# Conv and pooling states turned in one run of nine transposes, and last conv rows turned back by groups, in a one-core hybrid decoder step

## The chip, the core and the metric

The kernel runs on one core of a Trainium2 chip. The metric is the device time of one execution in microseconds (us). The kernel before took 1273.08 us, the median of three runs (1272.99 to 1273.53).

## What is computed

One layer of a decoder with two branches: a pooling branch, and a Mamba-2 branch with a short causal conv in front of it. There are 1024 prompt rows and 8 sequences of 8 sample rows, 1088 in all, D = 1024, everything in fp32. Each sample sequence brings the last 15 input rows of its pooling branch (`state_pool`, 8 x 15 rows of 512) and the last 3 raw rows of its conv (`state_conv`, 8 x 3 rows of 3072); the prompt brings none. Of both branches the last rows are outputs again. Cut to what matters here:

```python
def layer(x, c, pos0, pool_buf, conv_buf, ssm_state, ...):
    h = rmsnorm(x) * (1 + scale) + shift
    u_pool, z_pool, z_ssm, xbc, dt_raw, g_raw = split(h @ w_in)
    p, pool_new = pool_mix(u_pool, pool_buf, ...)   # windows 2, 4, 8, 16 over concat([pool_buf, u_pool])
    p = (p * silu(z_pool)) @ w_pool_out             # pool_new: its last 15 rows
    xbc_c, conv_new = causal_conv(xbc, conv_buf, conv_w, conv_b)   # 4 taps over concat([conv_buf, xbc])
    xs, B, C = split(silu(xbc_c))                   # conv_new: the last 3 rows of the concatenation
    y, ssm_new = ssd(xs, softplus(dt_raw + dt_bias), -exp(a_log), B, C, ssm_state)
    s = rmsnorm((y + d_skip * xs) * silu(z_ssm)) @ w_ssm_out
    x = x + gate * ((sigmoid(g0) * p + sigmoid(g1) * s) @ w_o)
```

## The kernel before

Activations stand turned: channels on the 128 partitions, rows (time) along the free axis. The product with `w_in` is made pair by pair: `pair` computes two blocks of 128 output channels for all rows by Strassen's method, seven products of two halves, each half 12 matmuls, since each fp32 operand is split into a high and a low part (L609 high times high, L610 high weight times low activation, L611 low weight times high activation). A pair is 168 matmuls of 272 columns, some 21 us of TensorE (PE). PSUM tiles come in turn from two sets, `mm` and `ps`; the `ps` set has five buffers and also takes every transpose.

The weights of a pair are loaded raw on the queue of SyncE (SP) (L541, or L544 where the two blocks don't lie side by side; tiles `rawA`, five buffers), combined on VectorE (DVE) (L555, tiles `raw`), and split by ScalarE (ACT) into the high part (`whi`, L166) and by GpSimd (POOL) into the low one (`wlo`, L169), four buffers of each.

Over a pair's matmuls lies the work of the unit that takes its results: a generator, stepped between products. The stages that matter:

- From 0 to about 95 us: `first`, in an order written by hand: modulation, norm, and the activations' halves.
- From about 95 to 545 us: the stage of the change. Its units are `to_conv` (which opens a pool of SBUF tiles, among them `GA`, seven buffers), one pair of `light` (z or gate channels), `pool_rows` (a DRAM-to-DRAM copy of old pool rows, on SP), then the pairs of `heavy` and `light` in turn: a pool pair (`upair`), then for each of four groups two x pairs, one B/C pair, and a further pool pair.
- From 545 us: dt is read back and turned (L1090 loads `s` on SP, L1109 turns it in nine transposes, one run), then the samples' recurrence beside the last `light` pairs to about 800, the chunks of the prompt to about 1160, and the tail of output products.

In the stage of the change no order is written by hand: a scheduler places instructions by its own estimate of time, engine by engine, in program order where priorities are equal. `behind(engine)` ties an instruction to a place: not ahead of the last one that the program has issued on that engine.

Beside these pairs `splits` prepares the later weights: loaded on ACT's queue (L427), scaled and copied by ACT, subtracted by POOL, the high part stored on ACT's queue, the low part on SP's (L442, `wp` and `ws`), in a place fixed by `behind(SP)`; the raw tile (`pw`) has two buffers.

`conv_unit(mc, dst)` is made for each of 24 blocks of 128 channels: 16 of x, 4 of B, 4 of C. It loads the block's 24 state rows as a 24 x 128 tile (L1033, SP, tag `stc`, four buffers), turns it on PE (L1039), and ACT copies the 24 columns (L1040) ahead of the samples' rows in a `GA` tile. When the pair's results stand there, ACT copies the last three columns of each sequence and of the prompt into `t27` (L1049 and the line behind it); ACT and DVE make the conv (L1054, L1057), ACT the Silu, and the results are stored on ACT's queue (L1064, L1065). Then PE turns the 27 columns back (L1067), ACT copies them out of PSUM (L1069), and two stores on ACT's queue (L1070, L1071) bring them to the outputs.

`u_unit(gi)` does the like for each of four pool blocks: 120 state rows loaded (L760, SP), turned (L775) and copied by DVE (L776); at the end two turns (L805 the prompt's 15 columns, L806 the samples' 64), two ACT copies and two stores on ACT's queue.

Of the kernel before, what the change touches and what calls it, by code (L numbers as in the profile page):

```python
# [20 lines left out]
P = 128  # L21
# [3 lines left out]
NB = 8  # L25
# [21 lines left out]
def tile_pool_ssd_step(  # L47
# [9 lines left out]
    def nm(s):  # L57
        uid[0] += 1
        return f"{s}_{uid[0]}"
# [36 lines left out]
    def PB():  # L96
        return psB.tile([P, 512], F32, tag="ps", name=nm("ps"))
# [38 lines left out]

    act(rc[:, 0:1], eps, AF.Silu)
    nc.gpsimd.memset(rc[:, 0:1], 1.0)
    vb = sm.tile([44, P], F32, tag="stc", name="vb", bufs=4)
    store_(vb[0:16, :], b_ada[0, 0:2048].rearrange("(m p) -> m p", p=P))  # L140
    store_(vb[16:24, :], norm_g[0].rearrange("(m p) -> m p", p=P))
    store_(vb[24:40, :], ssm_norm_g[0].rearrange("(m p) -> m p", p=P))
# [227 lines left out]
    cvT = pa.tile([P, 120], F32, tag="cvT", name="cvT")  # L370

    def late_loads():
        va = sm.tile([120, P], F32, tag="stc", name="va", bufs=4)
        load(va[0:96, :], conv_w[0].rearrange("k (m p) -> (k m) p", p=P))
        load(va[96:120, :], conv_b[0].rearrange("(m p) -> m p", p=P))
        V.memset(dtb, 0.0)
        load(dtb[0:NH, 0:1], dt_bias[0].rearrange("(h o) -> h o", o=1))
        dk = sm.tile([16, 2], F32, tag="rsm", name="dk")
        load(dk, d_skip[0].rearrange("(m h) -> m h", h=2))
        yield  # L380
        dx = sm.tile([16, 2, 64], F32, tag="stc", name="dx", bufs=4)
# [374 lines left out]

    def u_unit(gi):
        L = gi + 1
        stp = sm.tile([120, P], F32, tag="stc", name=nm("stp"), bufs=4)
        load(stp, state_pool[0, :, :, gi * P:(gi + 1) * P].rearrange("b t c -> (b t) c"))  # L760
        pwt = sm.tile([P, P], F32, tag="stc", name=nm("pwt"), bufs=4)
        load(pwt, pool_w[0, gi])
        yield
        up = GA([P, CW_])
        us = small([P, NB, 23], "us", 1)

        def done(o, n, comb, buf):
            e = min(o + n, SEQ) - o
            comb(up[:, 15 + o:15 + o + e], 0, e)
            if e < n:  # L770
                comb(us[:, :, 15:23], e, n, lambda t: t.rearrange("p (b t) -> p b t", t=8))
        yield done
        V.memset(up[:, 0:15], 0.0)
        ps = PB()
        nc.tensor.transpose(ps[:, :120], stp, ident[:120, :120])  # L775
        V.tensor_copy(us[:, :, 0:15], ps[:, :120].rearrange("p (b t) -> p b t", t=15))  # L776
        u64 = sm.tile([P, NB, 8], F32, tag="rsm", name=nm("u64"))
        act(u64, us[:, :, 15:23], AF.Copy)
        u15 = sm.tile([P, 27], F32, tag="t27", name=nm("u15"))
        act(u15[:, 0:15], up[:, SEQ:SEQ + 15], AF.Copy)  # L780
        yield
        a, av = up, us
        ab = [GA([P, T]) for _ in range(2)]
        for l in range(L):
            st = 1 << l
            o0 = 2 * st - 1
            b = ab[l % 2]
# [17 lines left out]
        nc.tensor.transpose(ps[:15, :P], u15[:, 0:15], ident)  # L805
        nc.tensor.transpose(ps[:NS, P:2 * P], u64.rearrange("p b t -> p (b t)"), ident)  # L806
        o15, o64 = [sm.tile([n, P], F32, tag="o27", name=nm("o15")) for n in (15, NS)]
        act(o15, ps[:15, :P], AF.Copy)
        act(o64, ps[:NS, P:2 * P], AF.Copy)
        store_(new_pool_p[0, 0, :, gi * P:(gi + 1) * P], o15)  # L810
        store_(new_pool_s[0, :, 7:15, gi * P:(gi + 1) * P], o64)
        y = up[:, :T]
        for o, n in BLK:
            ps = PB()
            mm(ps[:, :n], pwt, d[:, o:o + n], start=True, stop=True)
            act(y[:, o:o + n], ps[:, :n], AF.Copy, scale=pscl[:, gi:gi + 1])
        yp_[gi] = y
        yield 1
# [209 lines left out]

    def conv_unit(mc, dst):
        stc = sm.tile([24, P], F32, tag="stc", name=nm("stc"), bufs=4)
        load(stc, state_conv[0, :, :, mc * P:(mc + 1) * P].rearrange("b t c -> (b t) c"))  # L1033
        yield
        rp = GA([P, CW_])
        seg = rp[:, SEQ + 3:CW_].rearrange("p (b t) -> p b t", t=11)
        V.memset(rp[:, 0:3], 0.0)
        ps = PB()
        nc.tensor.transpose(ps[:, :24], stc, ident[:24, :24])  # L1039
        act(seg[:, :, 0:3], ps[:, :24].rearrange("p (b t) -> p b t", t=3), AF.Copy)  # L1040

        def done(o, n, comb, buf):
            e = min(o + n, SEQ) - o
# [1 line left out]
            if e < n:  # L1045
                comb(seg[:, :, 3:11], e, n, lambda t: t.rearrange("p (b t) -> p b t", t=8))
        yield done
        t27 = sm.tile([P, 27], F32, tag="t27", name=nm("t27"))
        act(t27[:, 0:24].rearrange("p (s t) -> p s t", t=3),  # L1049
            rp[:, SEQ:SEQ + 88].rearrange("p (s t) -> p s t", t=11)[:, :, 0:3], AF.Copy)  # L1050
        act(t27[:, 24:27], rp[:, SEQ + 88:SEQ + 91], AF.Copy)
# [11 lines left out]
        act(s64, d[:, SEQ + 3:CW_].rearrange("p (b t) -> p b t", t=11)[:, :, 0:8], AF.Silu)  # L1063
        store_(dst[:, :SEQ], d[:, :SEQ])  # L1064
        store_(dst[:, SEQ:], s64.rearrange("p b t -> p (b t)"))  # L1065
        ps = PB()
        nc.tensor.transpose(ps[:27, :P], t27, ident)  # L1067
        o27 = sm.tile([27, P], F32, tag="o27", name=nm("o27"))
        act(o27, ps[:27, :P], AF.Copy)  # L1069
        store_(new_conv_p[0, 0, :, mc * P:(mc + 1) * P], o27[0:3])  # L1070
        store_(new_conv_s[0, :, :, mc * P:(mc + 1) * P], o27[3:27])  # L1071
        yield 1

    H0B = 4
# [478 lines left out]
    def to_conv():  # L1553
        nonlocal right
        right.__exit__(None, None, None)
        right = tc.tile_pool(name="ga", bufs=1, side="right", reuse_waits="tile")
        gas.append(right.__enter__())

    def to_ssd():
        nonlocal right, sd, sp, mask, maskS, blkS, dtT, acT, wdT, wd3, blk3, Elb  # L1560
# [20 lines left out]
            load(new_pool_s[0, :, 0:7, :], state_pool[0, :, 8:15, :])  # L1581

    first()
    units = [plain(to_conv), light[1], plain(pool_rows)]
    units += weave(heavy, light[2:-LAST])
    pre = splits()
    units.append(plain(lambda: [None for _ in pre]))
# [262 lines left out]

    def m_split(k, mem):

        sh = sm.tile([P, P], F32R, tag="stc", name=nm("sh"), bufs=4)
# [201 lines left out]
```

## Time and profile before

| what | before |
|---|---|
| median of three runs | 1273.08 us |
| profiled execution | 1271.29 us |
| its span in the trace | 1269.5 us |
| PE busy | 1242.3 us, 98% |
| DVE, ACT, POOL busy | 900.9, 718.0, 683.1 us |
| DMA | 234.90 MB, mean 185 GB/s |
| granted clock, mean | 0.997 |
| PE rows that turn states or last rows | 24 + 24 + 4 + 8 = 60 |

The span is what the trace covers; the execution's own time is 1.8 us more, and the median of the unprofiled runs another 1.8. Busy times are sums of durations without overlaps, so an engine at 98% has hardly a gap; the table by stretches says where its gaps lie. Rows of matmuls give start, duration, engine, line and shape; matmuls overlap, so a duration is more than what one instruction takes from the engine. The profile counts some matmul rows less than the program has (9771 of them are in the trace).

### The profile page before, as it was taken

How to read it: one execution, taken by the hardware profiler on the slowest of the kernel's cores; microseconds unless marked ns; L12 is line 12 of the kernel's file. 1: busy time of each engine (PE TensorE's matmuls, PEld its weight loads, DVE VectorE, ACT ScalarE, POOL GpSimd, SP SyncE). 2: the span in 40 equal slices, each digit the busy share in tenths (PEclk: the TensorE clock that was granted, in tenths of full speed). 3: DMA queues.
4: the chain of work that ended last, by engine and by line, in shares of the span. 5: the costliest groups of instructions: out<-in, count | busy, mean ns of one | idle time of the engine just before them, and what ended most of it. 6: DMA issues, size and time to landing. Idle time of an engine off the chain costs nothing. (4 is left out here: it accounts for less than half of the span.)

```text
span 1269.5 us, 26341 instructions
## 1 busy us (share of the span) xinstructions
PE 1242.3 (98%) x9771; PEld 1173.9 (92%) x9771; DVE 900.9 (71%) x1584; ACT 718.0 (57%) x1683; POOL 683.1 (54%) x555
## 2 busy tenths in 40 slices
PE   7999999999999999999999999999999999999997
PEld 6779999999999999998989999999999999999786
DVE  4695678966979588975756665598677879766543
ACT  4665356474666656554554554687887768522211
POOL 1007669886878777764344454365565646545000
PEclk9999999999999999999999999999999999999999
DMA  9937354565456454443557445899766567485431
GB/s 332 298 104 226 116 167 161 181 204 160 138 182 201 146 182 164 149 138 116 157 142 226 151 147 167 283 300 319 217 200 201 181 212 206 152 291 179 149 108 50
DMA packets 225729, 234.90 MB, mean 185 GB/s; under 512 B 30369, under 2 KB 177009, under 8 KB 225594
## 3 DMA queue, kind: packets, MB, share of 16 engines
q1 hardware_dynamic: 155808, 159.01, 40.3%
q10 hardware_dynamic: 69794, 74.22, 17.4%
q8 instruction: 77, 1.26, 0.4%
q14 instruction: 50, 0.41, 0.1%
HBM read 158.67 MB, written 74.62 MB: 184 GB/s over the span
## 5 line engine op out<-in xcount | busy, mean ns | idle before, releaser
L169 POOL TENSOR_TENSOR wlo<-rawA,whi 128x512 fp32r<-128x512 f32 x120 | 189.0, 1580 | 170.5 <-ACT whi L166 95.8
L169 POOL TENSOR_TENSOR wlo<-raw,whi 128x512 fp32r<-128x512 f32 x92 | 155.1, 1693 | 122.2 <-ACT whi L166 119.3
L360 PE MATMUL mm<-Y,whi 128*128 128x352 f32 (+1 forms) x480 | 159.8, 333 | 0.7
L361 PE MATMUL mm<-Y,whi 128*128 128x352 f32 (+1 forms) x480 | 157.3, 328 | 0.4 <-DVE Y L1516 0.4
L362 PE MATMUL mm<-Y,wlo 128*128 128x352 f32 (+1 forms) x480 | 156.8, 327 | 0.0
L609 PE MATMUL mm<-Y,whi 128*128 128x272 f32 x496 | 146.3, 295 | 2.2 <-ACT whi L166 2.2
L611 PE MATMUL mm<-Y,wlo 128*128 128x272 f32 x496 | 143.5, 290 | 2.5 <-POOL wlo L169 2.0
L609 PE MATMUL ps<-Y,whi 128*128 128x272 f32 x496 | 143.8, 290 | 0.0
L610 PE MATMUL ps<-Y,whi 128*128 128x272 f32 x496 | 143.0, 288 | 0.0
L610 PE MATMUL mm<-Y,whi 128*128 128x272 f32 x496 | 142.9, 288 | 0.0
L611 PE MATMUL ps<-Y,wlo 128*128 128x272 f32 x496 | 142.5, 287 | 0.0
L1057 DVE SCALAR_TENSOR_TENSOR GA<-GA,cvT,GA 128x1112 f32<-128x1112 f32 x72 | 126.6, 1763 | 0.1
L166 ACT ACTIVATE whi<-rawA 128x512 fp32r<-128x512 f32 x125 | 78.1, 627 | 81.1 <-PE ps L610 44.0
L166 ACT ACTIVATE whi<-raw 128x512 fp32r<-128x512 f32 x96 | 58.9, 627 | 97.6 <-DVE raw L555 51.7
L609 PEld LDWEIGHTS mm<-Y,whi 128*128 128x128 f32 x496 | 93.5, 189 | 4.2 <-ACT whi L166 2.8
L611 PEld LDWEIGHTS mm<-Y,wlo 128*128 128x128 f32 x496 | 93.5, 189 | 2.9 <-POOL wlo L169 2.2
L360 PEld LDWEIGHTS mm<-Y,whi 128*128 128x128 f32 x480 | 90.3, 188 | 4.2 <-DVE G L1890 2.4
L610 PEld LDWEIGHTS mm<-Y,whi 128*128 128x128 f32 x496 | 93.5, 189 | 0.7 <-issue 0.6
L610 PEld LDWEIGHTS ps<-Y,whi 128*128 128x128 f32 x496 | 93.3, 188 | 0.4
L609 PEld LDWEIGHTS ps<-Y,whi 128*128 128x128 f32 x496 | 93.3, 188 | 0.2
L611 PEld LDWEIGHTS ps<-Y,wlo 128*128 128x128 f32 x496 | 93.4, 188 | 0.0
L361 PEld LDWEIGHTS mm<-Y,whi 128*128 128x128 f32 x480 | 90.3, 188 | 2.6 <-DVE Y L1516 0.9
(464 smaller groups left out, 3821.9 us busy)
## 6 DMA issues: line engine op xcount, KB each, us to landing
rawA<-in_w_in SPq DMA_DIRECT2D x46, 512.0 KB
dec<-acs_d SPq DMA_DIRECT2D x32, 512.0 KB
xbc<-GA ACTq DMA_DIRECT2D x24, 512.0 KB
xb<-xbc SPq DMA_DIRECT2D x32, 384.0 KB
rawA<-in_w_in SPq DMA_DIRECT2D x32, 256.0 KB
pw<-in_w_ssm_out ACTq DMA_DIRECT2D x32, 256.0 KB
ws<-ph ACTq DMA_DIRECT2D x32, 256.0 KB
ws<-pw SPq DMA_DIRECT2D x32, 256.0 KB
```

What stands on the lines that cost most here:

```text
L166: ins = act(hi[:, :, :ncols], raw[:, :, :ncols], AF.Copy)
L169: (eng or nc.gpsimd).tensor_tensor(lo[:, :, :ncols], raw[:, :, :ncols], hi[:, :, :ncols].bitcast(F32), ALU.subtract)
L360: mm(ps[:, :n], a, rh[k][:, o:o + n], start=(k == 0), stop=False)
L361: mm(ps[:, :n], a, rl[k][:, o:o + n], start=False, stop=False)
L362: mm(ps[:, :n], b, rh[k][:, o:o + n], start=False, stop=(k == nk - 1))
L609: mm(p, hi, ah, start=(k == 0), stop=False)
L610: mm(p, hi, al, start=False, stop=False)
L611: mm(p, lo, ah, start=False, stop=(k == 3))
L1057: V.scalar_tensor_tensor(d[:, :n], rp[:, k:k + n], cvT[:, 24 * k + mc:24 * k + mc + 1], d[:, :n], ALU.mult, ALU.add)
```

## The change

The states are no longer loaded by blocks of channels. In `to_conv` each state is loaded whole, into a `GA` tile: seen as rows of 128 channels, `state_conv` has 8 x 3 x 24 = 576 rows and `state_pool` 8 x 15 x 4 = 480, and 128 rows at a time stand on the partitions (four DMAs on SP, behind what SP has by then). A new unit `turn_states` behind the first `light` pair turns them in nine transposes (four of 128 rows and one of 64; three of 128 and one of 96) into three PSUM tiles, and ACT copies these into `st576` and `st480`, which stay. A `conv_unit` takes its 24 columns from `st576` by one strided ACT copy, a `u_unit` its 120 from `st480` by one strided DVE copy. The tag `stc` has three buffers instead of four.

The last rows: in `u_unit` the 15 and the 64 columns stand in one tile, `u79`, turned at once, copied at once, and stored by two stores on ACT's queue as before. In `conv_unit` the 27 columns of a group's six blocks stand side by side in one tile; the last of the six turns them in two transposes (108 and 54 columns), with an ACT copy each, and the twelve stores go to SP's queue, each pair of them behind what SP has been given by then, one pair per step.

The diff, without four further lines that only set `bufs=3` for `stc`:

```diff
@@ u_unit
-        stp = sm.tile([120, P], F32, tag="stc", name=nm("stp"), bufs=4)
-        load(stp, state_pool[0, :, :, gi * P:(gi + 1) * P].rearrange("b t c -> (b t) c"))
-        pwt = sm.tile([P, P], F32, tag="stc", name=nm("pwt"), bufs=4)
+        pwt = sm.tile([P, P], F32, tag="stc", name=nm("pwt"), bufs=3)
...
-        ps = PB()
-        nc.tensor.transpose(ps[:, :120], stp, ident[:120, :120])
-        V.tensor_copy(us[:, :, 0:15], ps[:, :120].rearrange("p (b t) -> p b t", t=15))
-        u64 = sm.tile([P, NB, 8], F32, tag="rsm", name=nm("u64"))
-        act(u64, us[:, :, 15:23], AF.Copy)
-        u15 = sm.tile([P, 27], F32, tag="t27", name=nm("u15"))
-        act(u15[:, 0:15], up[:, SEQ:SEQ + 15], AF.Copy)
-        yield
+        V.tensor_copy(us[:, :, 0:15], pool_t[0].rearrange("p (b t m) -> p b t m", t=15, m=4)[:, :, :, gi])
+        yield
+        u79 = sm.tile([P, 79], F32, tag="u79", name=nm("u79"), bufs=1)
+        act(u79[:, 15:].rearrange("p (b t) -> p b t", t=8), us[:, :, 15:23], AF.Copy)
+        act(u79[:, 0:15], up[:, SEQ:SEQ + 15], AF.Copy)
...
-        nc.tensor.transpose(ps[:15, :P], u15[:, 0:15], ident)
-        nc.tensor.transpose(ps[:NS, P:2 * P], u64.rearrange("p b t -> p (b t)"), ident)
-        o15, o64 = [sm.tile([n, P], F32, tag="o27", name=nm("o15")) for n in (15, NS)]
-        act(o15, ps[:15, :P], AF.Copy)
-        act(o64, ps[:NS, P:2 * P], AF.Copy)
-        store_(new_pool_p[0, 0, :, gi * P:(gi + 1) * P], o15)
-        store_(new_pool_s[0, :, 7:15, gi * P:(gi + 1) * P], o64)
+        nc.tensor.transpose(ps[:79, :P], u79, ident)
+        o79 = sm.tile([79, P], F32, tag="o79", name=nm("o79"), bufs=1)
+        act(o79, ps[:79, :P], AF.Copy)
+        store_(new_pool_p[0, 0, :, gi * P:(gi + 1) * P], o79[0:15])
+        store_(new_pool_s[0, :, 7:15, gi * P:(gi + 1) * P], o79[15:79])
@@ conv_unit
+    t27s = {}
...
-        stc = sm.tile([24, P], F32, tag="stc", name=nm("stc"), bufs=4)
-        load(stc, state_conv[0, :, :, mc * P:(mc + 1) * P].rearrange("b t c -> (b t) c"))
...
-        ps = PB()
-        nc.tensor.transpose(ps[:, :24], stc, ident[:24, :24])
-        act(seg[:, :, 0:3], ps[:, :24].rearrange("p (b t) -> p b t", t=3), AF.Copy)
+        act(seg[:, :, 0:3], conv_t[0].rearrange("p (b t m) -> p b t m", t=3, m=24)[:, :, :, mc], AF.Copy)
...
-        t27 = sm.tile([P, 27], F32, tag="t27", name=nm("t27"))
+        g, i = (mc // 4, mc % 4) if mc < 16 else (mc % 4, mc // 4)
+        if not i:
+            t27s[g] = sm.tile([P, 6 * 27], F32, tag="t27", name=nm("t27"))
+        t27 = t27s[g][:, 27 * i:27 * i + 27]
...
-        ps = PB()
-        nc.tensor.transpose(ps[:27, :P], t27, ident)
-        o27 = sm.tile([27, P], F32, tag="o27", name=nm("o27"))
-        act(o27, ps[:27, :P], AF.Copy)
-        store_(new_conv_p[0, 0, :, mc * P:(mc + 1) * P], o27[0:3])
-        store_(new_conv_s[0, :, :, mc * P:(mc + 1) * P], o27[3:27])
+        if i == 5:
+            ps = PB()
+            o27 = sm.tile([108, 2 * P], F32, tag="o27", name=nm("o27"))
+            for c, n in ((0, 108), (1, 54)):
+                nc.tensor.transpose(ps[:n, c * P:c * P + P], t27s[g][:, 108 * c:108 * c + n], ident)
+                act(o27[:n, c * P:c * P + P], ps[:n, c * P:c * P + P], AF.Copy)
+            for j, m in enumerate((4 * g, 4 * g + 1, 4 * g + 2, 4 * g + 3, 16 + g, 20 + g)):
+                r, c = j % 4 * 27, j // 4 * P
+                with behind(mybir.EngineType.SP):
+                    load(new_conv_p[0, 0, :, m * P:(m + 1) * P], o27[r:r + 3, c:c + P])
+                    load(new_conv_s[0].rearrange("b t c -> (b t) c")[:, m * P:(m + 1) * P], o27[r + 3:r + 27, c:c + P])
+                yield
@@ to_conv
+        for src, rows in ((state_conv, 576), (state_pool, 480)):
+            flat = src[0].rearrange("b t (m p) -> (b t m) p", p=P)
+            st, full = GA([P, 5, P]), rows // P
+            with behind(mybir.EngineType.SP):
+                load(st[:, :full], flat[:full * P].rearrange("(a r) p -> r a p", r=P))
+            with behind(mybir.EngineType.SP):
+                load(st[:rows - full * P, full], flat[full * P:])
+            states.append((st, rows))
+
+    def turn_states():
+        for (st, rows), kept_in in zip(states, (conv_t, pool_t)):
+            out = small([P, rows], "st%d" % rows, 1)
+            for a in range(0, rows, 512):
+                ps = PB()
+                e = min(rows, a + 512)
+                for r in range(a, e, P):
+                    n = min(P, e - r)
+                    nc.tensor.transpose(ps[:, r - a:r - a + n], st[:n, r // P], ident[:n, :n])
+                act(out[:, a:e], ps[:, :e - a], AF.Copy)
+            kept_in.append(out)
+    states, conv_t, pool_t = [], [], []
...
-    units = [plain(to_conv), light[1], plain(pool_rows)]
+    units = [plain(to_conv), light[1], plain(turn_states), plain(pool_rows)]
```

How this moves instructions is shown at three places. The first is PE between the first `light` pair and the pool pair behind it: `ps` and `mm` are PSUM tiles, `Y` the activations' halves, `whi` and `wlo` the split weights. Before:

```order
L609 MATMUL ps_1590<-Y_484,whi_1349 128x272
L610 MATMUL ps_1590<-Y_485,whi_1349 128x272
L611 MATMUL ps_1590<-Y_484,wlo_1350 128x272
L609 MATMUL mm_1632<-Y_484,whi_1315 128x272
L610 MATMUL mm_1632<-Y_485,whi_1315 128x272
L611 MATMUL mm_1632<-Y_484,wlo_1316 128x272
```

The same place of the changed kernel, where `GA_1301` holds the conv state and `GA_1304` the pool state:

```order
L610 MATMUL ps_1594<-Y_485,whi_1353 128x272
L611 MATMUL ps_1594<-Y_484,wlo_1354 128x272
L1575 MATMUL ps_1617<-ident,GA_1301 128x128 x4
L1575 MATMUL ps_1623<-ident,GA_1301 128x64
L1575 MATMUL ps_1627<-ident,GA_1304 128x128 x3
L1575 MATMUL ps_1627<-ident,GA_1304 128x96
L609 MATMUL mm_1649<-Y_484,whi_1321 128x272
L610 MATMUL mm_1649<-Y_485,whi_1321 128x272
```

The nine turns stand in one run between two pairs; the turns inside the units (L1039 and L775 of before) are gone, and the rest of the order here is that of before.

The second place is SP's queue in about the first 100 us, where the states are loaded in the changed kernel; `gate_d` is a store of the modulation, `rawA` are raw weights of `w_in`, and the last row is the copy of `pool_rows`:

```order
L760 DMA pwt_3996<-in_pool_w 128x128
L850 DMA gate_d<-bg 9x256 x4
L544 DMA rawA_1318<-in_w_in 128x4x128 x2
L541 DMA rawA_1634<-in_w_in 128x4x256
L1562 DMA GA_1301<-in_state_conv 128x4x128
L1564 DMA GA_1301<-in_state_conv 64x128
L1562 DMA GA_1304<-in_state_pool 128x3x128
L1564 DMA GA_1304<-in_state_pool 96x128
L442 DMA wp_177<-pw_1389 128x512
L1602 DMA out<-in_state_pool 8x3584
```

The four loads stand behind the two `rawA` loads; before, the first small state loads stood ahead of `gate_d`, and nothing stood between `rawA` and L442.

The third place is SP's queue at the end of the stage, where the last group's rows go out. Before (`s` is dt, `hst` the first chunk's input):

```order
L442 DMA ws_216<-pw_7176 128x512
L541 DMA rawA_7481<-in_w_in 128x4x256
L541 DMA rawA_7798<-in_w_in 128x4x256
L541 DMA rawA_7800<-in_w_in 128x4x256
L1090 DMA s_7465<-dts_d 128x1024
L1091 DMA s_7466<-dts_d 128x64
L1094 DMA A<-in_a_log 128x32
L1226 DMA hst_8140<-xbc_169 128x6x64
```

In the changed kernel, from the last of the six pairs of stores on (the other five stand right ahead of it):

```order
L1069 DMA out<-o_1114_7226 3x128
L1070 DMA out<-o_1114_7226 24x128
L1090 DMA s_7268<-dts_d 128x1024
L1091 DMA s_7269<-dts_d 128x64
L1094 DMA A<-in_a_log 128x32
L541 DMA rawA_7603<-in_w_in 128x4x256
L1226 DMA hst_7943<-xbc_169 128x6x64
L541 DMA rawA_7903<-in_w_in 128x4x256
```

The twelve stores stand ahead of the dt loads, and one of the weight loads that stood ahead of these now stands behind them.

More of the change, by code (lines that the diff above doesn't have):

```diff
@@ L138, in tile_pool_ssd_step @@
     nc.gpsimd.memset(rc[:, 0:1], 1.0)
-    vb = sm.tile([44, P], F32, tag="stc", name="vb", bufs=4)
+    vb = sm.tile([44, P], F32, tag="stc", name="vb", bufs=3)
     store_(vb[0:16, :], b_ada[0, 0:2048].rearrange("(m p) -> m p", p=P))
@@ L372, in late_loads @@
     def late_loads():
-        va = sm.tile([120, P], F32, tag="stc", name="va", bufs=4)
+        va = sm.tile([120, P], F32, tag="stc", name="va", bufs=3)
         load(va[0:96, :], conv_w[0].rearrange("k (m p) -> (k m) p", p=P))
@@ L380, in late_loads @@
         yield
-        dx = sm.tile([16, 2, 64], F32, tag="stc", name="dx", bufs=4)
+        dx = sm.tile([16, 2, 64], F32, tag="stc", name="dx", bufs=3)
         V.tensor_copy(dx, dk.unsqueeze(2).to_broadcast([16, 2, 64]))
@@ L1851, in m_split @@
     def m_split(k, mem):
-        sh = sm.tile([P, P], F32R, tag="stc", name=nm("sh"), bufs=4)
+        sh = sm.tile([P, P], F32R, tag="stc", name=nm("sh"), bufs=3)
         act(sh[:, 0:NS], acc[k][:, SEQ:], AF.Copy)
```

## The prediction

> **What bounds the kernel now.** I read the page's busy table first, then the table by stretches, then the waits of SP. The busy table has TensorE (PE) at 98% of the span; that is an average, so the stretches decide.
>
> ```profile
> PE 1242.3 (98%) x9771; PEld 1173.9 (92%) x9771; DVE 900.9 (71%) x1584; ACT 718.0 (57%) x1683; POOL 683.1 (54%) x555
> ```
> ```profile
> 95.00:145.00 50.00, 50.00 (x401) 49.83 (x400) 28.15 (x53) 24.34 (x51) 34.18 (x25) 1.00 0.55 174
> 145.00:540.00 395.00, 395.00 (x3111) 389.34 (x3111) 319.78 (x476) 231.29 (x554) 308.14 (x180) 1.00 0.52 169
> 540.00:800.00 260.00, 254.13 (x2204) 244.60 (x2203) 164.32 (x394) 135.24 (x288) 123.44 (x105) 0.99 0.53 158
> ```
>
> All edits lie between 95 and about 545 us. There PE is busy for 50.00 of 50.00 and 395.00 of 395.00 us, at a granted clock of 1.00, while ACT works 231.29 us, DVE 319.78 and POOL 308.14. So an instruction taken from PE there is taken from the time, whole, as long as nothing new makes PE wait; time taken from ACT, DVE or SP is worth nothing by itself. After that PE idles 5.9 us up to 800.
>
> A busy share does not price an instruction, because matmuls overlap. The price is the distance from start to start. In an undisturbed run of the main products:
>
> ```profile
> 181.04 0.29 PE L611 MATMUL mm<-G,wlo 128*128 128x272 f32 x1
> ...
> 189.05 0.29 PE L609 MATMUL ps<-Y,whi 128*128 128x272 f32 x1
> ```
>
> These two rows are 64 matmuls apart: 8.01 / 64 = 0.125 us each, though each "lasts" 0.29.
>
> **What leaves PE.** The counts of each kind (L806 runs as often as L805, right behind it):
>
> ```profile
> L1039 PE MATMUL ps<-ident,stc x24: 213/226/238, 144.8 to 496.8; 24*128 24x24 f32 x24
> L1067 PE MATMUL ps<-ident,t x24: 271/271/272, 177.7 to 539.4; 128*27 128x128 f32 x24
> L775 PE MATMUL ps<-ident,stp x4: 266/267/268, 144.6 to 451.3; 120*128 120x120 f32 x4
> L805 PE MATMUL ps<-ident,u x4: 271/272/272, 166.2 to 466.9; 128*15 128x128 f32 x4
> ```
> ```profile
> 169.99 0.29 PE L611 MATMUL mm<-Y,wlo 128*128 128x272 f32 x1
> 170.21 0.30 PE L1039 MATMUL ps<-ident,stc 24*128 24x24 f32 x2
> ...
> 170.79 0.29 PE L611 MATMUL mm<-Y,wlo 128*128 128x272 f32 x1
> ```
>
> Left out here are one L609 and one L610, so from L611 to L611 it would be 3 x 0.125 = 0.375 us without the pair of conv state turns (L1039); it is 0.80, so a pair costs 0.425. In the same way around one turn of the last conv rows (L1067), and between two turns of the pool rows:
>
> ```profile
> 177.55 0.29 PE L611 MATMUL ps<-Y,wlo 128*128 128x272 f32 x1
> 177.67 0.27 PE L1067 MATMUL ps<-ident,t 128*27 128x128 f32 x1
> ...
> 178.03 0.29 PE L611 MATMUL mm<-R,wlo 128*128 128x272 f32 x1
> ```
> ```profile
> 166.17 0.27 PE L805 MATMUL ps<-ident,u 128*15 128x128 f32 x1
> 166.28 0.27 PE L806 MATMUL ps<-ident,u 128*64 128x128 f32 x1
> ```
>
> 0.48 - 0.375 = 0.105 for the conv rows, 0.11 for a pool turn; L775, a pool state turn of 120 rows, I price like these. The narrow 24-row turns are thus the dear ones, 0.21 each. Sum removed: 12 x 0.425 = 5.10, 24 x 0.105 = 2.52, 4 x 0.11 = 0.44, 8 x 0.11 = 0.88; together **8.9 us**.
>
> **What comes to PE**: nine state turns (L1575 of the changed kernel), eight turns of the last conv rows (L1064) and four of the pool rows, 21 in all. The nearest existing row is nine turns in one run, eight of them 128 wide:
>
> ```profile
> 551.67 0.29 PE L610 MATMUL mm<-G,whi 128*128 128x272 f32 x1
> 551.80 1.14 PE L1109 MATMUL ps<-ident,s 128*128 128x128 f32 x9
> ...
> 553.03 0.29 PE L611 MATMUL ps<-R,wlo 128*128 128x272 f32 x1
> ```
>
> 1.36 - 0.375 = 0.985 us, 0.11 each. Two of the nine state turns have short blocks (64 and 96 rows). Their form is not in the trace; the nearest is the 24-row pair, which costs 0.425 - 2 x 0.11 = 0.2 us over its two turns' plain price. Bounds: 0 (short rows cost nothing) to 0.4 (both pay it); I take 0.2, as only the 64-row block is half empty. So 9 x 0.11 + 0.2 = 1.2; 8 x 0.11 = 0.9; 4 x 0.11 = 0.4; together **2.5 us**, bounds 2.3 to 2.7. Net: 8.9 - 2.5 = **6.4 us off PE**.
>
> [...]
>
> ```profile
> L1067 PEld LDWEIGHTS ps<-ident,t x24: 103/103/103, 177.6 to 539.3; 128*27 128x27 f32 x24
> L1109 PEld LDWEIGHTS ps<-ident,s x9: 111/141/142, 551.7 to 552.6; 128*128 128x128 f32 x8, 128*64 128x64 f32 x1
> ```
>
> The load does grow, 103 to 141 ns, but the starts stay 0.11 us apart in both, so it hides; I charge nothing and keep 21 x 0.038 = 0.8 us as a rival.
>
> **Off the path.** ACT copies: 24 of 27 rows become 8, eight pool copies out of PSUM become four, three state copies are new, and the 24 small conv copies stay with another source; DVE keeps its four pool copies. ACT and DVE have over 160 and 70 us free in 145 to 540, which covers them; without it, by the copies' own kind (L652 below, 0.39 us for 272 columns), the three state copies of 512, 64 and 480 columns would be under 2 us. They hold three of the five PSUM buffers of their kind until ACT has them out, and the two blocks hold two of the seven GA buffers until PE has turned them; both are free again long before the units that follow need them, since the first pair of conv units stands a whole unit (21 us) later.
>
> The state loads stand on SP behind a weight load that is issued here, and PE reaches their turns where the first row of the next unit stands:
>
> ```profile
> 98.94 0.37 SPq L541 DMA_DIRECT2D rawA<-in_w_in  x1
> ```
> ```profile
> 123.60 0.29 PE L609 MATMUL mm<-Y,whi 128*128 128x272 f32 x1
> ```
>
> 24 us for half a MB, so PE should not wait. ACT loses 48 store issues and SP gains them, losing 28 small loads and getting four large: 24 more issues net. One costs about this much, on either queue:
>
> ```profile
> 225.30 0.34 ACTq L1071 DMA_DIRECT2D out<-o  x1
> ```
>
> Twelve stores are 4.1 us of SP, with a wait for ACT's copy ahead; behind them stand weight loads. Their cover:
>
> ```profile
> 241.23 0.40 SPq L541 DMA_DIRECT2D rawA<-in_w_in  x1
> ```
> ```profile
> 270.75 0.68 DVE L555 TENSOR_TENSOR raw<-rawA,rawA 128x512 f32<-128x512 f32 x1
> ```
>
> The load at 241.23 is the one ahead of which the first group's stores come; by the order of before, the DVE row at 270.75 is the first to read what it brings, 29.5 us later. A burst of 4.1 us, or twice that, is hidden. If that cover were gone, a burst would cost up to its 4.1 us.
>
> The tight place is the last group, whose stores now come ahead of the loads for dt:
>
> ```profile
> 523.50 22.34 SPq L541 DMA_DIRECT2D rawA<-in_w_in  x3
> 545.94 0.45 SPq L1090 DMA_DIRECT2D s<-dts_d  x1
> ```
> ```profile
> 543.98 0.39 ACT L652 ACTIVATE s<-ps 128x272 f32<-128x272 f32 x1
> ```
> ```profile
> 548.00:550.00 2.00, 2.00 (x18) 2.00 (x17) 0.60 (x2) 0.63 (x1) 1.70 (x5) 1.00 1.05 392
> ```
>
> In the clock of before: the last group is turned where the last L1067 stands, at 539.4, and copied by ACT within a us; eight stores follow to about 543.5; the second copy stands on ACT behind L652 (ends 544.4) and two store issues (0.7), so it ends at 545.4; four stores, 1.4; then the dt load at 546.8 instead of 545.9. But the 512 KB weight load that went just ahead of it now goes behind, which at 392 GB/s is 1.3 us. It lands no later, and L1109 at 551.80 does not wait. What is late next, if so, is that weight load, by some 3 us, with the cover above.
>
> **The sum.** The profiled execution took 1271.29 us for a span of 1269.5; 1271.29 - 6.4 = 1264.9. The median of the runs shown, 1273.08, is 1.8 above it, and 1273.08 - 6.4 = **1266.7 us**, 0.5% less. 0.2% is 2.5 us, about what a measurement of this kernel can tell from no change; the bound lies at 1270.5.
>
> **Rivals.** That the change doesn't do what it says is none here: the order has the 60 turns gone and the 21 in place.
> - The last group's chain is late. For: the second copy waits on ACT behind Silu work that itself waits for DVE. Against: the order of loads. If dt comes 3 us late PE stands 3 us at L1109: 1269.7, at the edge of the bound. Chance 0.10.
> - The wide loads show: 6.4 - 0.8 = 5.6, so 1267.5. Chance 0.06.
> - More: one PE wait of 2.0 us sits at 600.9, where POOL is behind.
>
> ```profile
> PE mm L611 <- POOL wlo L169: 2.0, 1, 2.0
> ```
>
>   If the shifted stage meets it better: 1264.7. Chance 0.07.
> - The gain is swallowed behind 545, where PE already has 5.9 us of waits: the samples' chain is started by loads on SP, which do not move up with PE if SP is later. The waits then grow by what PE gained, less some: 1272, no change. Against: PE is full until 600. Chance 0.10.
> - Slower: ACT is held, not SP. A later load of raw weights on ACT's queue needs a buffer that an SP store frees; in the second group that SP store now stands behind the twelve. ACT stands in order, and what it stands before are the weight splits.
>
> ```profile
> L169 POOL TENSOR_TENSOR wlo<-rawA,whi 128x512 fp32r<-128x512 f32 x120 | 189.0, 1580 | 170.5 <-ACT whi L166 95.8
> ```
> ```profile
> ACT whi L166 <- PE ps L610: 68.0, 55, 4.8
> ```
>
>   ACT's splits wait for PE to free one of four buffers, 55 times, and run then; so three products of 24 matmuls (9 us) are the cover, less 1.6 for POOL's subtraction and about 1 for the split: it decides from a stop of 6.4 us. If all four groups stopped ACT so that PE lost the 4.1 us of a burst each: 16.4 - 6.4 = 10 us more, 1283. Chance 0.09.
>
> **How the numbers follow.** Forecast 0.58. Faster by over 0.2%: 0.58 + 0.06 + 0.07 + half of 0.10 = 0.76; within 0.2%: 0.05 + 0.10 = 0.15; slower 0.09. Range: below it reaches the extra gain and a us of scatter, 1263.5; above it takes in the late chain and the swallowed gain, 1273.5; it leaves out the slow case and scraps.
>
> **What would show it.** PE still full in 95 to 545, with 21 turns in that stretch; the nine L1575 in one run at 0.11 with no idle before them; L1109 about 6 us earlier without a wait; L1109's dt load issued some 1 us nearer to it. Wrong would be: a wait of PE for L1575's loads or dt, a DVE wait for a weight load, or the steps after 600 at their old times.

## The result, and the profile after

The changed kernel takes 0.9966 of the time of the kernel before, with a 95% interval of 0.9954 to 0.9978: medians of twelve runs each, 1270.00 us against 1274.25, so 4.3 us less (2.8 to 5.9). Two later measurements of both kernels gave 0.9951 (0.9934 to 0.9968) and 0.9965 (0.9949 to 0.9980). Forecast were 6.4 us less; the time lies in the range, and faster was forecast with 0.76.

The busy row of the page after, and the table by stretches (columns: the stretch, its length, then busy time and instructions of PE, PEld, DVE, ACT and POOL, the granted clock, DMA share and GB/s):

```profile
PE 1238.8 (98%) x9732; PEld 1173.2 (93%) x9732; DVE 907.8 (72%) x1584; ACT 715.8 (56%) x1666; POOL 683.7 (54%) x555
```
```profile
145.00:540.00 395.00, 395.00 (x3122) 392.21 (x3121) 329.69 (x477) 231.42 (x539) 315.95 (x183) 1.00 0.51 167
540.00:800.00 260.00, 253.22 (x2194) 243.47 (x2193) 165.31 (x396) 134.34 (x285) 120.86 (x104) 0.99 0.53 161
```

PE is still busy for all of 145 to 540, so the new turns and stores brought it no wait of note there. To read the stage itself, take its two ends in each trace: the row at which the states are turned, or would be, and the first turn of dt. Between them every variant but `rows_act` has the same 3290 main products. After:

```profile
124.49 0.29 PE L611 MATMUL ps<-Y,wlo 128*128 128x272 f32 x1
124.62 1.36 PE L1575 MATMUL ps<-ident,GA 128*128 128x128 f32 x9
125.76 0.37 PE L609 MATMUL mm<-Y,whi 128*128 128x272 f32 x1
125.97 0.29 PE L610 MATMUL mm<-Y,whi 128*128 128x272 f32 x1
...
546.65 1.03 PE L1109 MATMUL ps<-ident,s 128*128 128x128 f32 x8
```

546.65 - 124.62 = 422.03 us; before it was 551.80 - 123.60 = 428.20 (rows of the prediction). The stage is 6.2 us shorter. The nine state turns cost 125.97 - 124.49 = 1.48, less two plain starts of 0.125: 1.23. Three of the nine rows by themselves:

```profile
125.14 0.27 PE L1575 MATMUL ps<-ident,GA 64*128 64x64 f32 x1
```
```profile
125.35 0.33 PE L1575 MATMUL ps<-ident,GA 128*128 128x128 f32 x1
```
```profile
125.73 0.25 PE L1575 MATMUL ps<-ident,GA 96*128 96x96 f32 x1
```

From the first turn at 124.62 to the one behind the 64-row block (125.35) five starts take 0.73 us instead of 5 x 0.108 = 0.54; the three from there to the 96-row block take 0.38 instead of 0.33. The 96-row block stands 0.24 us ahead of the L610 behind it (125.97), as the plain turn at 177.67 of the prediction does (178.03 - 0.125 = 177.91). So the 64-row block costs some 0.25 us more than a plain turn and the 96-row block nothing more. One turn of a group's last rows, in the same way:

```profile
232.89 0.29 PE L611 MATMUL ps<-Y,wlo 128*128 128x272 f32 x1
233.02 0.27 PE L1064 MATMUL ps<-ident,t 128*108 128x128 f32 x1
...
233.25 0.29 PE L610 MATMUL mm<-Y,whi 128*128 128x272 f32 x1
```

0.36 - 0.25 = 0.11 us for 108 columns. The one turn that is left of each pool block stands 0.11 us ahead of the next matmul too. SP's end of the stage, on its own queue:

```profile
541.26 0.30 SPq L1070 DMA_DIRECT2D out<-o  x1
541.67 0.35 SPq L1090 DMA_DIRECT2D s<-dts_d  x1
...
543.07 0.38 SPq L541 DMA_DIRECT2D rawA<-in_w_in  x1
```

The dt load goes out 546.65 - 541.67 = 4.98 us ahead of its turn, before 551.80 - 545.94 = 5.86; PE does not wait for it.

But the span shrank by only 1.6 us in this pair of profiles. The head is part of that: the stage begins at 124.62 instead of 123.60, and ahead of that PE's order is that of before. Behind the stage more is lost. The first turn of the chunks, before and after:

```profile
810.01 0.29 PE L118 MATMUL ps<-identR,xb 128*128 128x128 f32 x2
```
```profile
806.26 0.22 PE L118 MATMUL ps<-identR,xb 128*128 128x128 f32 x1
```

It comes 810.01 - 806.26 = 3.75 us earlier, 4.77 with the head's 1.02 taken out; so 1.4 of the 6.2 went in the samples' stage. About as much again went near 1110, where eleven products in a row take (1113.56 - 1110.03) / 11 = 0.32 us each; in before products of this width start 0.17 us apart (1121.44 to 1121.61, for one).

```profile
1110.03 0.53 PE L360 MATMUL mm<-Y,whi 128*128 128x384 f32 x1
...
1113.56 0.39 PE L362 MATMUL mm<-Y,wlo 128*128 128x384 f32 x1
```

In the samples' stage one wait stands out, for the product `dec` (L1275, a subtraction on DVE), before and after:

```profile
629.53 0.50 PE L1291 MATMUL ps<-dec,dec 96*128 96x512 f32 x1 [0.64 <-DVE dec L1275]
```
```profile
621.84 0.28 PE L610 MATMUL mm<-G,whi 128*128 128x272 f32 x1
624.77 0.50 PE L1291 MATMUL ps<-dec,dec 96*128 96x512 f32 x1 [2.65 <-DVE dec L1275]
...
626.18 0.43 PE L609 MATMUL mm<-G,whi 128*128 128x272 f32 x1
...
628.68 0.43 PE L611 MATMUL ps<-Y,wlo 128*128 128x272 f32 x1
629.07 0.29 PE L610 MATMUL ps<-Y,whi 128*128 128x272 f32 x1
```

PE waits 2.65 us, and the starts behind the wait stand (628.68 - 626.18) / 11 = 0.227 us apart instead of 0.125: thirteen products at about half speed, 1.3 us more. The granted clock (third number from the end) reads 0.50 there and 1.00 ahead of the wait:

```profile
615.00:622.00 7.00, 6.86 (x56) 6.52 (x54) 3.23 (x7) 2.34 (x7) 0.65 (x2) 1.00 0.67 204
626.00:628.00 2.00, 2.00 (x11) 2.00 (x10) 1.46 (x6) 0.37 (x1) 0.00 (x0) 0.50 0.27 86
```

I took this for the place where the gain goes (theory A below). The head and the stretch near 1110 I took for chance.

### The profile page after: what moved, and what is told of

Read it like the earlier page. It is cut to its first block, busy times and chain, and to the rows that moved or that the text cites. A ratio compares the mean times of both kernels' runs of the same rounds, so it can differ in the third digit from the quotient of the medians.

```text
span 1267.9 us, 26167 instructions
## 1 busy us (share of the span) xinstructions
PE 1238.8 (98%) x9732; PEld 1173.2 (93%) x9732; DVE 907.8 (72%) x1584; ACT 715.8 (56%) x1666; POOL 683.7 (54%) x555
## 3 DMA queue, kind: packets, MB, share of 16 engines
q8 instruction: 77, 1.26, 0.4%
## 5 line engine op out<-in xcount | busy, mean ns | idle before, releaser
L169 POOL TENSOR_TENSOR wlo<-rawA,whi 128x512 fp32r<-128x512 f32 x120 | 193.6, 1619 | 159.9 <-ACT whi L166 80.4
L169 POOL TENSOR_TENSOR wlo<-raw,whi 128x512 fp32r<-128x512 f32 x92 | 149.4, 1630 | 125.4 <-ACT whi L166 83.7
L611 PE MATMUL mm<-Y,wlo 128*128 128x272 f32 x496 | 143.9, 291 | 1.8 <-POOL wlo L169 1.3
L610 PE MATMUL ps<-Y,whi 128*128 128x272 f32 x496 | 143.3, 289 | 0.0
L611 PE MATMUL ps<-Y,wlo 128*128 128x272 f32 x496 | 143.1, 288 | 0.0
L610 PE MATMUL mm<-Y,whi 128*128 128x272 f32 x496 | 142.5, 288 | 0.0
L166 ACT ACTIVATE whi<-rawA 128x512 fp32r<-128x512 f32 x125 | 78.0, 626 | 84.4 <-PE ps L610 46.6
L166 ACT ACTIVATE whi<-raw 128x512 fp32r<-128x512 f32 x96 | 58.8, 627 | 81.3 <-DVE raw L555 51.5
L611 PEld LDWEIGHTS mm<-Y,wlo 128*128 128x128 f32 x496 | 93.2, 188 | 2.4 <-POOL wlo L169 1.5
L610 PEld LDWEIGHTS mm<-Y,whi 128*128 128x128 f32 x496 | 93.5, 188 | 0.7 <-issue 0.6
L610 PEld LDWEIGHTS ps<-Y,whi 128*128 128x128 f32 x496 | 93.6, 189 | 0.4
L611 PEld LDWEIGHTS ps<-Y,wlo 128*128 128x128 f32 x496 | 93.4, 188 | 0.0
```

The source lines that it names most:

```text
L166: ins = act(hi[:, :, :ncols], raw[:, :, :ncols], AF.Copy)
L169: (eng or nc.gpsimd).tensor_tensor(lo[:, :, :ncols], raw[:, :, :ncols], hi[:, :, :ncols].bitcast(F32), ALU.subtract)
L610: mm(p, hi, al, start=False, stop=False)
L611: mm(p, lo, ah, start=False, stop=(k == 3))
```

## Experiments

**The two kernels once more, unchanged** (`again_before`, `again_after`), to know what one program's profiles differ by.

> The kernel before, unchanged, once more: what two executions of one program differ by. Theory A (the change takes about 6.2 us out of the stretch up to the turns of dt, 2 us of that go to a longer PE wait for the samples' DVE product near 622 us, and the rest of the small profiled difference of 1.65 us is chance: a head that was 1.0 us slower and a stretch of matmuls at half speed near 1110 us that cost 1.6): ratio 1.000 within 0.002; from the row of PE where the states would be turned to the first turn of dt 428.2 us within 0.3; the head up to there differs from the first profile by up to 1 us. Rival B (the profiled difference is what the change is worth, all of it structural): the head and the places of half speed are those of the first profile of before within 0.2 us.

> The changed kernel, unchanged, once more. Theory A: 422.0 us within 0.3 from the first turn of the states to the first turn of dt, 6.2 less than before; the PE wait for the samples' DVE product near 622 us is there again at some 2.6 us (before 0.6), since nothing in it is chance; the half-speed stretch near 1110 us is gone or elsewhere; ratio 0.9966 again, 0.9955 to 0.998. Rival B: the same 1.6 us are lost near 1110 us, and the ratio lies at 0.9987.

Before: ratio 0.9999 (0.9979 to 1.0020); the stage is 554.15 - 125.78 = 428.37, so the head ended 2.2 us later than in the first profile and the stage agrees to 0.2. After: 0.9951 (0.9934 to 0.9968); 545.25 - 123.22 = 422.03 again, and 2.65 us of wait near 622 again, while before has 0.40. There is no half-speed stretch near 1110 this time. Rival B falls: the 1.65 us of the first pair was a poor measure. Theory A stood, for now.

**Each part alone.** `states_only` keeps the last rows' code of before, `rows_only` the states' code of before:

```diff
 states_only, conv_unit against the changed kernel:
-        if not i:
-            t27s[g] = sm.tile([P, 6 * 27], F32, tag="t27", name=nm("t27"))
-        t27 = t27s[g][:, 27 * i:27 * i + 27]
+        t27 = sm.tile([P, 27], F32, tag="t27", name=nm("t27"))
...
+        nc.tensor.transpose(ps[:27, :P], t27, ident)
 rows_only, conv_unit against the changed kernel:
+        load(stc, state_conv[0, :, :, mc * P:(mc + 1) * P].rearrange("b t c -> (b t) c"))
...
+        nc.tensor.transpose(ps[:, :24], stc, ident[:24, :24])
```

> The states loaded whole and turned in one run, the last rows turned back block by block as before. Theory A, by the terms of the prediction (12 pairs of narrow turns at 0.425 and 4 pool state turns at 0.11 go, nine at 1.2 in all come): 5.10 + 0.44 - 1.2 = 4.3 us off the stretch up to the turns of dt, 423.9 instead of 428.2; ratio 0.9965 to 0.998. Rival C (the wide turns or the wait for the large loads cost what the narrow ones did): 427 to 428, ratio 0.9995.

> The last rows turned back by groups and stored from SP, the states loaded and turned as before. Theory A: 2.52 + 0.88 - 0.88 - 0.44 = 2.1 us off the stretch up to the turns of dt, 426.1 instead of 428.2; ratio 0.998 to 0.9995. Rival D (the twelve stores on SP delay the dt load or ACT's weights): less than 1 us off, or a wait of PE at the turns of dt.

Their stages, from the turns of the states (or the product that stands there) to the turns of dt:

```profile
124.71 0.27 PE L1569 MATMUL ps<-ident,GA 128*128 128x128 f32 x1
...
549.37 0.27 PE L1103 MATMUL ps<-ident,s 128*128 128x128 f32 x1
```
```profile
125.43 0.28 PE L609 MATMUL mm<-Y,whi 128*128 128x272 f32 x1
...
552.17 0.27 PE L1117 MATMUL ps<-ident,s 128*128 128x128 f32 x1
```

`states_only`: 424.66, 3.5 us off where 4.3 was expected; `rows_only`: 426.74, 1.5 off where 2.1 was. In the first, the one PE wait of the stage takes 0.4 us of the difference (PE for POOL's L169). Ratios: 0.9965 (0.9948 to 0.9982) and 0.9998 (0.9981 to 1.0014). The states are the larger part, as the terms had it; C and D fall for the stage. What `rows_only` gained there did not show in its time, for which 0.998 to 0.9995 was expected, though its interval reaches there: it too waited 2.44 us for `dec`.

**Why PE waits for `dec`.** The trace of after shows a chain. On DVE, L1275 stands behind a copy (L1284) for the next group, which waits for that group's load; POOL runs two weight splits (L169) at that moment:

```profile
622.29 0.65 DVE L1284 COPY cz<-hst 128x32 f32<-128x32 f32 x1 [0.88 <-DMA hst<-xbc]
622.97 1.75 DVE L1275 TENSOR_TENSOR dec<-xw,dec 32x512 fp32r<-32x512 f32 x1
```
```profile
621.63 1.27 POOL L169 TENSOR_TENSOR wlo<-rawA,whi 128x512 fp32r<-128x512 f32 x1 [6.35 <-ACT whi L166]
622.91 1.26 POOL L169 TENSOR_TENSOR wlo<-raw,whi 128x512 fp32r<-128x512 f32 x1
```

And in before:

```profile
628.42 0.34 DVE L1284 COPY cz<-hst 128x32 f32<-128x32 f32 x1 [1.22 <-DMA hst<-xbc]
628.79 0.68 DVE L1275 TENSOR_TENSOR dec<-xw,dec 32x512 fp32r<-32x512 f32 x1
```
```profile
627.44 1.28 POOL L169 TENSOR_TENSOR wlo<-rawA,whi 128x512 fp32r<-128x512 f32 x1 [4.90 <-ACT whi L166]
628.88 1.73 POOL L169 TENSOR_TENSOR wlo<-raw,whi 128x512 fp32r<-128x512 f32 x1 [0.16 <-ACT whi L166]
```

The same subtraction takes 0.68 us where it starts ahead of POOL's second split (which then takes 1.73) and 1.75 where it starts 0.06 us behind it, ending 0.55 us after POOL does. Who comes first hangs on ACT: in before POOL's second split waited 0.16 us for its high part (L166), in `again_before` 0.40 us, and DVE started in that gap; in all eight profiles with the long wait POOL's second split follows its first within 0.02 us. The longer subtraction is only part of the wait, 1.75 - 0.68 = 1.07 us of the 2.65. The rest is that DVE comes to the subtraction late: in after 0.85 us behind the time at which PE is ready for it (622.97 against 621.84 + 0.28 = 622.12), in before 0.10 us ahead (628.79 against 629.53 - 0.64 = 628.89). So two edits, each in the place of the wait. `cz_behind` keeps that copy behind its own group (and `cz_behind_before` does so in the kernel before); `sub_pool` gives the subtraction to POOL, in whose order it stands ahead of the two splits:

```diff
 cz_behind, cz_behind_before:
+            with behind(mybir.EngineType.DVE, 1):
                 V.tensor_copy(cz[:, :, 0:8], ...)
 sub_pool:
-            V.tensor_tensor(xh[64:96], xsf[64:96], xh[64:96].bitcast(F32), ALU.subtract)
+            nc.gpsimd.tensor_tensor(xh[64:96], xsf[64:96], xh[64:96].bitcast(F32), ALU.subtract)
```

> The changed kernel, with the copy of C's columns kept behind the DVE instruction that its own group issued ahead of it, so that the DVE product that PE waits for near 622 us no longer stands behind a copy of the next group, which waits for its load. Theory A (part of the gain is swallowed there: PE arrives earlier, DVE is held by that copy and then by POOL's split, PE waits 2.65 us instead of 0.4 to 0.64 and after it runs its matmuls at half speed for another 1.5 to 4 us): the wait falls to under 1.6 us, no half-speed stretch follows, and the kernel takes 2 to 4 us less than the changed one, some 1266; ratio to the kernel before 0.9915 to 0.994. Rival E (the wait is set elsewhere, by the chain of products ahead of it or by POOL alone): the wait stays within 0.4 of 2.65 and the time within 1 us of the changed kernel's.

> The same edit in the kernel before. Theory A: PE waits only 0.4 to 0.64 us there, so the edit is worth at most that: ratio 0.999 to 1.0005. If it is worth as much here as in the changed kernel (0.997 or less), the copy is a loss of both kernels and no part of why the change gained less than its turns.

> The changed kernel, with the subtraction that PE waits for near 622 us made by POOL instead of DVE, in POOL's order ahead of the two weight splits between which it was caught. Theory A: POOL is idle for 6 us ahead of them, so the product is ready about 622 us, PE waits less than 1 us there and does not slow down: 2 to 4 us less than the changed kernel, unless POOL's splits, some 1 us later each of eight times, hold PE elsewhere. Rival E: no change of that wait.

In `cz_behind` the wait is gone (0.9 us at the longest), so what Rival E says of it falls. But the time is 0.9948 (0.9931 to 0.9964), against the changed kernel's 0.9951 in the measurement before, so the 2 to 4 us of theory A did not come either. The waits of PE in its samples' stage:

```profile
PE mm L611 <- POOL wlo L169: 4.2, 3, 2.0
PE ps L1292 <- DVE dec L1275: 1.6, 3, 0.9
PE mm L609 <- ACT whi L166: 0.6, 2, 0.4
```

against 3.3 us for `dec` (three waits) and 1.3 us for POOL in after. POOL's splits now hold PE for what `dec` held it before, and ten products at half speed stand behind the longest of these waits. `cz_behind_before` gave 0.9984 (0.9966 to 1.0003); the interval holds what was expected if the edit is worth nothing and what was expected if it is worth as much as there, so it decides nothing. `sub_pool` gave 0.9930 (0.9911 to 0.9950), which looked like the 2 us, so it was run again beside the changed kernel, together with a third pair of profiles.

> The changed kernel with that one subtraction made by POOL, once more beside the changed kernel on the same chip: if the wait near 622 is worth what it lasts, 2 us less than the changed kernel in this call, ratio 0.993 to 0.9945; if another wait takes its place, within 1 us of it.

> The kernel before, a third profile beside the runs of this call. If the longer wait near 622 us belongs to the change (theory A), PE waits 0.4 to 0.7 us here for the samples' DVE product, with the second weight split of POOL behind that product; if it is chance (theory F), it may be 2.4 to 2.7 here too. From the turns of dt to the first turn of the chunks: 254 to 258 us.

> The changed kernel, a third profile beside the runs of this call: 422.0 us within 0.3 from the turns of the states to the turns of dt; by theory A the wait of 2.65 us near 622 again and 259 to 260 us from the turns of dt to the first turn of the chunks, 1.5 to 5 more than before; ratio 0.995 to 0.997, that is 4 to 6 of the 6.2 us.

`sub_pool_2`: 0.9962 (0.9945 to 0.9980), the changed kernel beside it 0.9965. Its wait for `dec` is 0.47 us, but PE now waits for ACT's split, 1.8 us in one place:

```profile
PE mm L609 <- ACT whi L166: 2.0, 2, 1.8
PE mm L611 <- POOL wlo L169: 1.6, 1, 1.6
PE mm L609 <- ACT dec L1202: 1.0, 1, 1.0
PE ps L1291 <- POOL dec L1275: 0.5, 1, 0.5
```

From the turns of dt to the first turn of the chunks `cz_behind` takes 259.1 us and the two profiles of `sub_pool` 257.8 and 257.9, the changed kernel 259.3 on the mean of three. So a wait taken out of this stage is not worth what it lasted: of 2.65 us and 1.3 at half speed at most 1.5 came back. Neither version beats the changed kernel by more than the measurement tells. `third_after` (1269.16 us) has its 2.65 us again, with a stage of 546.83 - 124.14 = 422.7, 0.4 of it one wait for ACT. But `third_before`, which is the kernel before without an edit, has the long wait as well:

```profile
630.10 1.74 DVE L1275 TENSOR_TENSOR dec<-xw,dec 32x512 fp32r<-32x512 f32 x1
```
```profile
630.04 1.26 POOL L169 TENSOR_TENSOR wlo<-raw,whi 128x512 fp32r<-128x512 f32 x1
```
```profile
631.90 0.51 PE L1291 MATMUL ps<-dec,dec 96*128 96x512 f32 x1 [2.38 <-DVE dec L1275]
```

POOL came 0.06 us ahead of DVE here too. That makes theory A's central claim, that the long wait belongs to the change, fall; theory F, chance, holds at least for before. From the turns of dt to the first turn of the chunks, the three profiles of before take 258.2, 254.5 and 260.2 us (254 to 258 was expected of the third), those of after 259.6, 259.8 and 258.4.

**The turns put back as such.** `plus_turns` adds 56 wide turns to the changed kernel; their results are not used, the outputs are made as before.

```diff
+        ps = PB()
+        for k in range(2 if mc % 3 else 3):
+            nc.tensor.transpose(ps[:, k * P:k * P + P], ident, ident)
         act(seg[:, :, 0:3], conv_t[0]...
```

> The changed kernel with 56 further turns of the identity, 128 wide, in the conv units; nobody reads their results. By the price of 0.11 us for a wide turn: 56 x 0.11 = 6.2 us, so 428.2 from the turns of the states to the turns of dt, as long as before. If a wide turn inside a unit costs what a narrow one did (0.21), 433.8. Theory A1 (the wait near 622 comes of PE's lead at the turns of dt): it is back at 0.4 to 0.7. Theory A2 (it comes of what stands where in the queues of SP and ACT about dt): it stays at 2.4 to 2.7.

```profile
145.48 0.29 PE L611 MATMUL ps<-Y,wlo 128*128 128x272 f32 x1
145.61 0.71 PE L1033 MATMUL ps<-ident 128*128 128x128 f32 x5
...
146.28 0.29 PE L610 MATMUL mm<-Y,whi 128*128 128x272 f32 x1
```

Five turns take 0.80 - 0.25 = 0.55 us, 0.11 each, and 56 of them 6.2. The stage is 553.13 - 123.33 = 429.8, 7.8 more than without, of which 0.8 are two short waits of PE (0.5 for POOL, 0.3 for DVE) and 0.7 the slower starts right behind them; 0.21 each would have made it 11.8. The time is 1.0015 (1.0000 to 1.0030) of the kernel before, the changed kernel beside it 0.9965: 0.5%, or 6.4 us, for 6.2 us of turns. With as late a PE as before, the wait for `dec` is 2.17, so A1 (PE's lead) falls too; A2 expected 2.4 to 2.7 and is not shown either.

**The stores on ACT's queue.**

```diff
-                with behind(mybir.EngineType.SP):
-                    load(new_conv_p[...], o27[r:r + 3, c:c + P])
-                    load(new_conv_s..., o27[r + 3:r + 27, c:c + P])
+                store_(new_conv_p[...], o27[r:r + 3, c:c + P])
+                store_(new_conv_s..., o27[r + 3:r + 27, c:c + P])
```

> The changed kernel, with the twelve stores of each group on ACT's queue instead of SP's. Theory A (PE alone sets the stage; SP's burst and ACT's are both covered): 422.0 us within 0.5 from the turns of the states to the turns of dt, time within 2 us of the changed kernel. Rival D (the place of the stores matters): ACT's 4.1 us for a group's stores hold its weight splits, and PE waits in that stretch: 424 us or more.

The ratio is 1.0069 (1.0051 to 1.0086): some 14 us more than the changed kernel by medians of two measurements (1284.27 and 1270.00), and 9 us more than the kernel before beside it (1275.32). From the turns of the states to the turns of dt it is 554.65 - 126.05 = 428.6, but here 26 main products that stand ahead of the turns of dt in the other variants come behind them (3264 in the stage instead of 3290). With these, 26 x 0.125 = 3.3 us, the same work takes 431.9, 9.8 us more than in after. Rival D holds. ACT's queue and PE at the first group:

```profile
244.91 1.03 ACTq L1068 DMA_DIRECT2D out<-o  x1
...
247.88 0.25 ACTq L1068 DMA_DIRECT2D out<-o  x1
248.17 0.31 ACTq L1069 DMA_DIRECT2D out<-o  x1
248.52 0.63 ACT L166 ACTIVATE whi<-rawA 128x512 fp32r<-128x512 f32 x1 [4.41 <-DMA out<-o]
...
249.06 0.38 ACT L652 ACTIVATE s<-mm 128x272 f32<-128x272 f32 x1
```
```profile
249.49 0.39 PE L609 MATMUL mm<-R,whi 128*128 128x272 f32 x1 [2.45 <-ACT s L652]
```

ACT stands 4.41 us before its split while it issues stores and waits between them, the copies out of PSUM (L652) come behind, and PE waits 2.45 us for a PSUM tile. Up to the turns of dt PE waits 4.3 us for such copies of ACT and 2.4 us for DVE, 6.7 of the 9.8 us, and sixteen products at half speed behind the wait shown (0.226 us from start to start) make 1.5 more; the rest I have not placed. The samples' stage then takes 268.2 us, 264.9 without the 26 products.

## Why the prediction was right, and where its size was off

- **What bounds the stage: right.** PE is busy throughout 145 to 540 in both kernels (395.00 of 395.00 us), and time taken from PE shows in the stage (6.2 of 6.4 us).
- **What leaves, what comes: right.** Forecast were 1.2 us for the nine state turns, measured 1.23, and the reason given for the 0.2 over nine plain turns holds too: the half-empty 64-row block pays it (0.25), the 96-row block does not. It also stands alone in its PSUM tile, but the change of tile at 124.62 cost nothing (0.13 us behind the L611 at 124.49, a plain start). Last rows 0.11 and pool rows 0.11, as forecast. The stage shrank by 6.2 of the 6.4 us. The parts alone gave 3.5 and 1.5; of the missing 1.2, 0.7 are a stop of PE at 222.51 in `states_only` (0.4 of it the wait for POOL's L169) and 0.3 a stop at 482.27 in `rows_only`, where PE's weight load waits for the same kind of split; the last 0.2 I can't place.
- **The wide loads hide: right.** The 56 added turns cost 0.11 each with a load of 140 ns (`plus_turns`). The 0.8 us of that rival did not show.
- **The stores on SP are covered: right, and the queue mattered more than the prediction said.** PE waits nowhere in the stage in two profiles of after, and 0.4 us in the third. The prediction counted ACT's relief at nothing, because ACT had time to spare; in the kernel before, with these 48 stores on ACT's queue two by two, PE has no wait in the stage either. But the same stores on ACT in groups of twelve cost some 14 us. A busy share says nothing of a burst: 4.4 us of ACT at one point left PE waiting 2.45 us for a PSUM tile in `rows_act`.
- **The last group's chain: right.** The dt load stands 4.98 instead of 5.86 us ahead of its turn, 0.9 nearer as worked out, and PE does not wait.
- **The step that was mis-sized is "The sum": it took all of the stage's gain to arrive at the end.** Measured were 4.3, 6.2 and 5.0 us by the medians of the three measurements (1274.25, 1274.58, 1274.18 against 1270.00, 1268.38, 1269.16). The three ratios, weighted by their intervals, give 0.9962 (0.9954 to 0.9970), that is 4.8 us (3.8 to 5.9), so some 1.4 us (0.3 to 2.4) of the stage's 6.2 did not arrive. (The forecast time itself, 1266.7, was low by a further 1.2 because the kernel before takes 1274.25 by twelve executions and not the 1273.08 of three.) The rival "the gain is swallowed behind 545" holds in part: by the three profiles of each, the samples' stage took 257.6 us on the mean before and 259.3 after, so 1.7 of the 6.2 went there. It did not go by the loads that the rival named: DVE's copy waited 0.88 us for its load in after and 1.22 in before. And before alone scatters over 5.7 us in that stage, so this difference is not shown by three profiles each. What is shown is how such a loss arises: DVE and POOL come within 0.1 us of each other, and where POOL is first DVE's product is 1.07 us later; with DVE's own lateness PE waits over 2 us, and mostly runs at half speed behind it. It went against the changed kernel three times in three, against the four variants that keep a part of it or add to it (`states_only`, `rows_only`, `plus_turns`, `rows_act`) each time, and against the kernel before once in three. Whether the change makes it likelier stays open. The rival of an extra gain at the POOL wait near 600 us was right in a small part: that wait lasts 2.0, 1.9 and 1.3 us in before and 1.3, 1.1 and 0.8 in after, 0.6 less on the mean.

## What to carry to other kernels

Price an instruction on a full engine by the distance of its neighbours' starts with and without it, and compare the stage between two fixed rows of the trace: 422.0 and 428.3 us came back within 0.7, while whole runs scattered over 6 us and more. Count the products between the two rows as well: in `rows_act` 26 were missing there, and the plain difference hid a third of the loss. Where the stage behind has waits of its own, a gain handed to it may be taken up there, and removing one of these waits may only bring up the next (1.8 us for ACT in `sub_pool_2`). Many small issues gathered into a burst need a queue on which nothing urgent stands behind them: in `rows_act` a weight split stood 4.41 us behind stores on ACT's queue.

## What the runs showed of the hardware that was not expected

- **DVE and POOL in each other's way.** DVE's subtraction of 32 x 512 took 0.68 us or 1.75, according to whether POOL's 128 x 512 subtraction had begun 0.06 us before it; when DVE was first, POOL's took 1.73 instead of 1.26. Of the sixteen such subtractions of DVE in before and after one took 1.75 us and the others 0.68. What makes them longer is not shown.
- **Half speed after a short wait.** Behind the waits of 2.17 to 2.65 us for `dec`, PE ran its products at about 0.227 us instead of 0.125 for 1.4 to 3.4 us in seven profiles of eight (`states_only` did not); in after the granted clock reads 0.50 there. Waits for POOL had such a stretch behind them too, 2.00 us in before (granted clock 0.50 from 604 to 607 us) and 2.0 us in `cz_behind` (ten products). How short a wait can be that has one is not shown. A like stretch near 1110 in after (granted clock 0.56 from 1110 to 1112 us) has no wait ahead of it. It follows eighteen products of one column each, and `third_before` has one as well, behind eighteen such products, so it is no part of the change; its cause is not shown.
